# Sparse attention beside a short convolution: attention's products moved into the array's halves and spread over all dense products

## The chip, the core and the metric

One Trainium2 chip, of which the kernel uses one core. The metric is the device time of one execution in microseconds; lower is better. The figure given for a kernel is the median of its runs.

## The reference, cut to what matters

One token sequence of 512 tokens with 1024 channels passes through one layer. An RMS norm feeds one input projection whose columns are split: queries (8 heads of 64), six key and value tensors (2 key groups of 64 each), 24 gates, and five stretches of 512 columns for the attention's gate path and the convolution.

```python
h = rms_norm(x, norm_w)
q, kv, gate_logits, z_attn, conv_h, conv_b, conv_c, z_conv = split(h @ w_in)
kc, vc = compress(k_cmp), compress(v_cmp)     # 31 overlapping blocks of 32 tokens, an MLP with SiLU
for branch in (compressed, selected, window): # each with its own keys and values
    p = masked_softmax(q @ k.T / 8 + t5_bias(distance))      # causal
    o += sigmoid(gate[branch]) * (p @ v)
conv = conv_b * causal_conv3(conv_c * conv_h)
mixed = concat([o * silu(z_attn), conv * silu(z_conv)])
out = rms_norm(x + mixed @ w_out, final_norm_w)
```

With 512 tokens there are 8 blocks of 64 to select from and 16 may be selected, so the selected branch is full causal attention, and so is the window of 512. Four heads share the keys of a group. All data are float32.

## The kernel before, in words

**Products.** Each float32 product is made of parts: a number is split into a rounded part (hi) and the rest (lo), and three passes are summed, hi by hi, hi by lo and lo by hi. A dense product takes 128 channels by 128 output columns by 512 tokens; a chunk of 128 output columns has 8 of those, 24 passes (`chunk_task`, lines 281 to 285). The weights come by a DMA of 512 KB that SP issues, ScalarE writes hi (L272) and GpSimd lo (L274), and an evacuation that differs by chunk empties the PSUM bank.

**The stream.** Dense work is a list of tasks (`Stream`). `st.fill(ns)` puts so many nanoseconds of dense passes into TensorE's order, `st.run(n)` finishes the n-th task; loads run two tasks ahead of splits, and splits some tasks ahead of the products. TensorE's order is the order in the program. At the start SP's order and those of ScalarE, VectorE and GpSimd are written out by hand as well; afterwards the framework orders these from its own estimate of when each instruction can run. The stream's order is: attention's gate chunks (za), the convolution's gate chunks (zc), two key chunks (selected and window), the values in three tasks of 32 products with 280 columns, four query chunks, twelve convolution chunks, the convolution's half of the output projection, and for each block of 128 tokens the attention's half and the final norm.

**The start.** Two chunks, the keys and values to be compressed, follow the channel blocks of the tokens as they land; squares of the tokens give the norm (R). After them come the compression's first layer (`hid`, L731), its sum, and its second layer. The compression's weights are split into two tensors, tagged `mixc` and `T`.

**The bias table.** `T` holds for each of 128 queries the bias of 8 heads at 512 distances. VectorE writes a row for each head (`vr`), a DMA writes 32 copies of it to DRAM (`vrd`), and four loads of 512 KB read these back skewed (L719). The table has the tag `T`, and so it can be loaded only when the hidden layer has read the weights of that tag.

**Attention.** Query blocks of 128 tokens run in the order 3, 2, 1, 0, each with two key groups, each group with two units (selected and window; block 0 has both in one): 14 units. A unit does four heads of one key group. For each head the two score passes (L825) have 128 rows, which are hi and lo of the query one below the other, against a hi and a lo stack of keys that is stored twice. VectorE adds the bias to the scores in PSUM and finds the largest (L764) and leaves the result in memory; ScalarE takes the exponential there (L830) and `weigh` multiplies by the inverse sum and the gate and writes two float16 parts (L851, L852). A DMA transposes these for each head (L854, 56 in all), and the values' products (L892) have 512 columns (4 heads by 128 tokens) and 128 output rows (hi and lo of the values one below the other). The compressed probabilities are turned on VectorE in 32 by 32 blocks (L871) and enter by one product with 64 rows (`pch`, `vcs`). `merge` adds the two halves and applies the gate path. Scores of unit n + 2 are laid between the values of unit n, a step at a time, with dense passes between the steps (`FILL`, `FILL_S`, `FILL_END`).

PSUM has eight banks: 2 for dense products, 4 for scores, 2 for the attention's output.

Of the kernel before, what the change touches and what calls it, by code (L numbers as in the profile page):

```python
# [30 lines left out]
C_KC, C_VC, C_KS, C_KW = 512, 640, 768, 1024  # L31
C_VS, C_VW = 896, 1152
C_ZA, C_H, C_B, C_C, C_ZC = 1304, 1816, 2328, 2840, 3352
CHUNKS = ([C_KC, C_VC] + [C_ZA + 128 * j for j in range(4)] + [C_ZC + 128 * j for j in range(4)]
          + [C_KS, C_KW] + [128 * j for j in range(4)] + [C_B + 128 * j for j in range(4)]
          + [c + 128 * j for j in range(4) for c in (C_H, C_C)])
CH = {c: i for i, c in enumerate(CHUNKS)}
OUT_ORDER = (6, 7, 0, 1, 2, 4, 5, 3)
FILL_LEAD = 3600
ON_POOL = (1, 1, 0, 0)  # L40
BANKS = {'proj': 2, 'S': 4, 'o': 2}
NP = 4
LATER = (2400, 2400)
WOA_DVE = (2,)
WARM = 8
LAG = 1
# first loads: channels of the tokens and weights of the first two chunks; then the stream (z), small ones (c) and
# the first weights of the compression (w)
STARTS = (0, (C_VC, 0, 2), (C_KC, 0, 2), 1, 2, (C_KC, 2, 4), (C_VC, 2, 5), 3, 4, (C_KC, 4, 5), 5, (C_KC, 5, 8),
          (C_VC, 5, 8), 6, 7)  # L50
LOADS = 'zzcwwwwwwzww'
# the engine of each channel block's squares, and the additions that follow
SQ = 'VAVAVAAA'
ADDS = ((), ((0, 1, 'P'),), (), ((2, 3, 'V'), (0, 2, 'P')), (), ((4, 5, 'V'), (0, 4, 'V')), ((0, 6, 'P'),),
        ((0, 7, 'V'),))
LAST = 384
Z_POOL = 2
CLO_DVE = (2, 3)
HID_AT = 4
KV_AT = 1  # L60
AHEAD = 3
# how much of the dense products is laid between the steps of a unit, unit by unit
FILL = (5600, 4432, 1229, 59, 4584, 1731, 1954, 4314, 3026, 2165, 3883, 4401, 4462, 1860)
FILL_FIRST = 800
FILL_S = 500
FILL_END = 1300
NW = 8
NCST = 237       # packed small parameters
NCP = 32         # copies of the bias rows that the skewed read goes through
VG = 280         # v_slc | v_win | gates  # L70
# [20 lines left out]
TC = dict(schedule_with_timeline_sim=True)  # L91


@with_exitstack
def hybrid_kernel(ctx: ExitStack, tc: tile.TileContext, xt0, xt, x, wt, wv, w1k, w1v, cst, rbr, wo, fnw, out):
# [4 lines left out]
    raw = ctx.enter_context(tc.tile_pool(name="raw", bufs=3))  # L100
    whl = ctx.enter_context(tc.tile_pool(name="whl", bufs=3))
# [11 lines left out]
    wraws = {}  # L113

    def load_w(c, a, b):
        if not a:
            wraws[c] = raw.tile([128, 8, 128], F32, tag="wraw", name=f"wraw{c}")
        nc.sync.dma_start(out=wraws[c][:, a:b], in_=wt[CH[c]][:, a:b])
# [3 lines left out]
    nws = xts[0][:, 0:NW]  # L122

# [4 lines left out]
    def load_xt(k):  # L128
        if k == 0:
            nc.sync.dma_start(out=xts[0][:, 0:NW + S], in_=xt0)  # L130
        else:
            nc.sync.dma_start(out=xk(k), in_=xt[k - 1])

    for what in STARTS:
        if isinstance(what, int):
            load_xt(what)
        else:
            load_w(*what)
    rbt = one.tile([NH, NB], F32, tag="tmpa", name="rbt")
    csts = one.tile([128, NCST], F32, tag="pct", name="csts")  # L140
# [4 lines left out]
    rms, cws = kept[:, 0:1], kept[:, 1:13].rearrange("p (j i) -> p j i", i=3)  # L145

    # two unit matrices, one below the other
# [9 lines left out]
    # has the table loaded that the squares and the inverse root share  # L157
    nc.scalar.activation(sm.tile([128, 1], F32, tag="ss", name="first"), epsb, AF.Abs_reciprocal_sqrt)
    ones = one.tile([128, 128], F32R, tag="pch", name="ones")
    nc.vector.memset(f32(ones), 1.0)  # L160
    vr = one.tile([NH, S], F32, tag="convu", name="vr")
    vneg = one.tile([NH, 128], F32, tag="pc", name="vneg")
    nc.vector.memset(vneg, NEG)

# [17 lines left out]
    def part_w(c, a, b, w):  # L182
        t, ks = wraws[c], slice(a, b)
        if not a:
            w.extend(whl.tile([128, 8, 128], F32R, tag=n, name=f"{n}{c}") for n in ("whi", "wlo"))
# [379 lines left out]
    for j in range(4):  # L565
        chunk_task(128 * j, queries_to(j))
# [428 lines left out]
```

## Time and profile before

| what | us |
|---|---|
| median of 3 runs | 322.18 |
| lowest and highest run | 321.29, 322.49 |
| span of the profiled execution, first to last instruction | 319.6 |
| TensorE busy | 276.4 |
| VectorE busy | 225.9 |
| ScalarE busy | 169.6 |
| GpSimd busy | 171.3 |

The profile is of one execution, 319.6 us from its first to its last instruction; the runs are timed from outside and have a median of 322.18 us. The ends of matmuls are modelled: the record of a dense product lasts about 0.4 us although the next one starts 0.23 us after it, so the distance of starts is the pace. Times of one line of the program can be those of several shapes; the number behind x counts instructions. Idle time is put down to what ended it.

### The profile page before, as it was taken

To read this page: it belongs to the slowest core of one execution; us is meant where nothing else is said; L and a number is where in the kernel's file an instruction comes from. 1 tells how busy PE (TensorE), PEld (TensorE's weight loads), DVE (VectorE), ACT (ScalarE), POOL (GpSimd) and SP (SyncE) were. 2 spreads that over 40 slices of the span, in tenths; PEclk is the share of its full clock that TensorE was granted. 3 is DMA by queue.
4 is the path that set the end of the run, shared out by engine and by line. 5 is a ranking of instruction groups with operands and counts; after the bars stand their busy time and mean duration, and the time that the engine had idled before them with its cause. 6 is when DMAs were issued, how large, how long until landed. Compare 5 with 4: busy or idle time off the path is not lost. (4 is left out here: it accounts for less than half of the span.)

```text
span 319.6 us, 4299 instructions
## 1 busy us (share of the span) xinstructions
PE 276.4 (86%) x1248; PEld 212.4 (66%) x1248; DVE 225.9 (71%) x582; ACT 169.6 (53%) x357; POOL 171.3 (54%) x160
## 2 busy tenths in 40 slices
PE   6979998990699999999998998798959895999792
PEld 5647877870588977888776756575737563677482
DVE  3998968010115358368978988699699999899773
ACT  5915455200325437358485485854745756576562
POOL 3894744540664354436746455575765785234710
PEclk9889999997699999999999999999979999999999
DMA  6767421469532242242866895597566652343413
GB/s 197 280 192 284 132 66 66 53 119 218 181 97 72 82 170 79 66 132 44 194 131 144 149 196 167 133 162 162 160 141 98 195 186 49 49 71 99 115 68 131
DMA packets 55400, 42.59 MB, mean 133 GB/s; under 512 B 43984, under 2 KB 46416, under 8 KB 55376
## 3 DMA queue, kind: packets, MB, share of 16 engines
q1 hardware_dynamic: 55376, 42.31, 52.1%
q8 instruction: 10, 0.16, 0.2%
q14 instruction: 14, 0.11, 0.1%
HBM read 29.06 MB, written 2.75 MB: 100 GB/s over the span
## 5 line engine op out<-in xcount | busy, mean ns | idle before, releaser
L274 POOL TENSOR_TENSOR wlo<-wraw,whi 128x512 fp32r<-128x512 f32 x52 | 69.7, 1362 | 58.6 <-ACT whi L272 47.1
L281 PE MATMUL ps<-hhi,whi 128*128 128x512 f32 x208 | 84.4, 406 | 12.1 <-ACT zc L299 11.2
L283 PE MATMUL ps<-hlo,whi 128*128 128x512 f32 x208 | 83.3, 401 | 0.0
L285 PE MATMUL ps<-hhi,wlo 128*128 128x512 f32 x208 | 82.8, 398 | 0.4 <-POOL wlo L274 0.4
L281 PEld LDWEIGHTS ps<-hhi,whi 128*128 128x128 f32 x208 | 39.8, 191 | 21.9 <-ACT zc L299 11.6
L852 DVE SCALAR_TENSOR_TENSOR p<-P,den,p 128x512 f16<-128x512 f32 (+3 forms) x64 | 46.3, 763 | 4.8 <-ACT p L851 4.7
L830 ACT ACTIVATE P<-P,mx 128x512 f32<-128x512 f32 (+3 forms) x64 | 35.5, 556 | 24.7 <-DVE mx L764 21.4
L272 ACT CAST whi<-wraw 128x1024 fp32r<-128x1024 f32 x26 | 27.0, 1043 | 38.9 <-DMA wraw<-in_wt 20.3
L285 PEld LDWEIGHTS ps<-hhi,wlo 128*128 128x128 f32 x208 | 39.6, 190 | 9.0 <-POOL wlo L274 0.8
L283 PEld LDWEIGHTS ps<-hlo,whi 128*128 128x128 f32 x208 | 39.8, 191 | 8.0
L851 ACT ACTIVATE p<-P,den 128x512 f16<-128x512 f32 (+3 forms) x56 | 27.9, 566 | 16.8 <-issue 10.2
L825 PE MATMUL s<-K,Q 128*128 128x512 f32 (+5 forms) x112 | 33.4, 380 | 0.0
L892 PE MATMUL o<-pt,V 128*128 128x512 f16 x80 | 24.6, 390 | 7.2 <-DMA pt<-p 5.1
L764 DVE CUSTOM_DVE_ANT_0 P<-s,T 128x512 f32<-128x512 f32 (+3 forms) x64 | 29.6, 483 | 0.2
L825 PEld LDWEIGHTS s<-K,Q 128*128 128x128 f32 x112 | 21.1, 194 | 6.8 <-issue 1.5
L294 DVE TENSOR_TENSOR ps<-ps,R 128x512 f32<-128x512 f32 x10 | 7.0, 696 | 20.4 <-PE ps L285 20.3
L471 PE MATMUL pc<-wochi,mc 128*128 128x512 f32 x32 | 13.3, 415 | 5.9 <-DVE y L478 3.3
L892 PEld LDWEIGHTS <-V 128*128 128x128 f16 x80 | 4.6, 98 | 18.2 <-issue 13.8
L533 PE MATMUL po<-woa,mahi 128*128 128x512 f32 (+1 forms) x36 | 13.4, 372 | 1.0 <-DVE y L540 1.0
L535 PE MATMUL po<-woa,mahi 128*128 128x512 f32 (+1 forms) x36 | 13.9, 386 | 0.0
L537 PE MATMUL po<-woa,malo 128*128 128x512 f32 (+1 forms) x36 | 13.4, 372 | 0.0
L475 PE MATMUL pc<-wochi,mc 128*128 128x512 f32 x32 | 12.9, 403 | 0.0
(190 smaller groups left out, 526.2 us busy)
## 6 DMA issues: line engine op xcount, KB each, us to landing
wraw<-in_wt SPq DMA_DIRECT2D x26, 512.0 KB, 3.5
wo<-in_wo SPq DMA_DIRECT2D x8, 512.0 KB, 3.8
T<-vrd SPq DMA_DIRECT2D x4, 512.0 KB, 9.5
xt<-in_xt SPq DMA_DIRECT2D x7, 256.0 KB, 4.8
out<-z SPq DMA_DIRECT2D x3, 512.0 KB, 2.7
w1r<-in_w1k SPq DMA_DIRECT2D x4, 256.0 KB, 5.2
w1r<-in_w1v SPq DMA_DIRECT2D x4, 256.0 KB, 7.1
y<-in_x SPq DMA_DIRECT2D x2, 512.0 KB, 3.5
```

Source lines behind the costliest of these rows:

```text
L272: nc.scalar.copy(hi, t)
L274: nc.gpsimd.tensor_sub(lo[:, ks], t[:, ks], f32(hi[:, ks]))
L281: nc.tensor.matmul(ps, hi[:, k, :], hhi[:, k, :], start=(k == 0), stop=False)
L283: nc.tensor.matmul(ps, hi[:, k, :], hlo[:, k, :], start=False, stop=False)
L285: nc.tensor.matmul(ps, lo[:, k, :], hhi[:, k, :], start=False, stop=(k == 7))
L535: nc.tensor.matmul(ps, mh[:, k, :], woa[1][:, k, ns], start=False, stop=False)
L764: nc.vector.tensor_tensor_reduce(out=dst, in0=src, in1=bias, scale=-1.0, scalar=3e38, op0=ALU.add, op1=ALU.min, accum_out=mx)
L825: nc.tensor.matmul(o, Q[h][:, gr.qs], k, start=(p == 0), stop=(p == 1))
L830: nc.scalar.activation(P, P, AF.Exp, bias=ngm, scale=-1.0, accum_out=self.su[:, 4 * i + hh:4 * i + hh + 1])
L851: nc.scalar.mul(p16[:, i, 0], P, c)
L852: nc.vector.scalar_tensor_tensor(out=p16[:, i, 1], in0=P, scalar=c, in1=p16[:, i, 0], op0=ALU.mult, op1=ALU.subtract)
L892: nc.tensor.matmul(gr.ob, v, p, start=(gr.n_pv == 1), stop=(gr.n_pv == 4 * gr.qb + 5))
```

## The change

The rows and columns of the tensor engine's array are used in halves by attention. Keys and queries are stored once, with the channels of the two key groups on partitions 0 to 63 and 64 to 127; the columns of the query and attention gate chunks are put together accordingly (heads j and j + 4). A unit now does two heads of each group. A score takes three passes with 64 rows, and the two groups' passes alternate, into two banks. The scores stay in PSUM: bias, exponential and weighting read and write there, two heads at a time. Values are three passes with 64 output rows and 256 columns, the two groups in the two halves of the rows of one bank; the split of the values lies beside, not below. Compressed probabilities of all 8 heads of a query block are weighted together, written in float16 parts and turned by a DMA.

The order: four chunks (compressed values, compressed keys, selected keys, window keys) follow the tokens at the start. Then come values, queries, and from there attention's units, one whole unit of values and one of scores at a time, with 7.5 to 12 us of dense passes between units, over gate chunks, convolution, and output projection. Query blocks run in the order 3, 2, 0, 1. The bias table has its own space and eight loads, among the first weights in SP's order; 16 copies of the rows instead of 32. The hidden layers' weights use one tensor in turn, values first. SiLU is computed as x (1 + tanh(x/2)) with the half put into later factors. The output projection of the convolution does one block of tokens after the other with all four channel blocks rather than two blocks half and half; the last two channel blocks of the convolution's result stay in PSUM for their split. Four raw and four split weight buffers replace three.

```diff
-OUT_ORDER = (6, 7, 0, 1, 2, 4, 5, 3)
-FILL = (5600, 4432, 1229, 59, 4584, 1731, 1954, 4314, 3026, 2165, 3883, 4401, 4462, 1860)
+START = (VC, KC, KS, KW)
+OUT_ORDER = (0, 1, 2, 3, 6, 7, 4, 5)
+BLOCKS = (3, 2, 0, 1)
+NW_RING = 4
+FILL = {3: 12000, 2: 10000, 0: 7500, 1: 7800}
+BEHIND = {10: 27}
...
     def silu_to(dst, conv=False):
         def evac(ps):
-            nc.scalar.activation(dst(), normed(ps), AF.Silu)
+            nc.vector.tensor_mul(dst(), ps, R)
+            th = one.tile([128, S], F32, tag="tanh", name="th")
+            nc.scalar.activation(th, dst(), AF.Tanh, scale=0.5)
+            nc.vector.scalar_tensor_tensor(out=dst(), in0=th, scalar=1.0, in1=dst(), op0=ALU.add, op1=ALU.mult)
...
+    def keys_to(br, ps):
+        normed(ps)
+        nc.scalar.copy(K[:, 0, br, 32:], ps)
+        nc.vector.tensor_sub(K[:, 1, br, 32:], ps, f32(K[:, 0, br, 32:]))
...
+            nc.scalar.copy(q2[:, 0], ps)
+            nc.vector.tensor_sub(q2[:, 1], ps, f32(q2[:, 0]))
...
-            y = hy[j][:, 1, :]
-            nc.vector.tensor_mul(y, ps, y)
+            y = ps if j in CLO_DVE else hy[j][:, 1, :]
+            nc.vector.tensor_mul(y, ps, hy[j][:, 1, :])
...
         def mms(w):
             wcs[kp] = w
-            for tb in range(2):
-                yield from block(tb, (kp,))
-            if kp:
-                for tb in range(2, 4):
-                    yield from block(tb, (0, 1))
+            for tb in range(4) if kp else ():
+                yield from block(tb)
...
+    with tc.manual_schedule(engines={mybir.EngineType.SP}):
+        st.fetch(1)
+        nc.sync.dma_start(out=vrd.rearrange("b h i -> h b i"), in_=vr.unsqueeze(1).to_broadcast([NH, NCP, 640]))
+        st.fetch(2)
+        load_w1(1)
+        st.fetch(4)
+        load_bias(range(0, 4))
+        st.fetch(5)
+        load_bias(range(4, 8))
+        st.fetch(6)
+        load_w1(0)
...
+        def start_mm(k, part):
+            for i, c in enumerate(START):
+                wh, wl = (t[:, k % 2, i * 128:(i + 1) * 128] for t in whs[k // 2])
...
+    ROWS = [slice(0, 64), slice(64, 128)]
+    PARTS = ((0, 0), (1, 0), (0, 1))
...
+        def product(self, v, p):
...
+            for g in range(2):
+                nc.tensor.matmul(self.ob[ROWS[g], 0:256], v(g), p(g), start=(self.n_pv == 1),
+                                 stop=(self.n_pv == 6 * (self.qb + 1) + 1))
+        def merge(self):
+            h0 = 2 * self.jj
+            self.product(lambda g: vcs[:, g], lambda g: self.cmp.pt[:, 4 * g + h0:4 * g + h0 + 2])
+            zs = za[:, h0:h0 + 2, self.qs]
+            nc.vector.scalar_tensor_tensor(out=zs, in0=self.ob[:, 0:256].rearrange("p (j t) -> p j t", j=2), scalar=vdn,
+                                           in1=zs, op0=ALU.mult, op1=ALU.mult)
...
+            for j2 in range(2):
+                q = Q[2 * gr.jj + j2]
+                s = [bank("S", f"s{nm}{j2}{g}")[:, 0:nb * W].rearrange("p (b c) -> p b c", b=nb) for g in range(2)]
+                for n, (a, b) in enumerate(PARTS):
+                    for g in range(2):
+                        nc.tensor.matmul(s[g], q[ROWS[g], a, gr.qs], K[ROWS[g], b, brs[0]:brs[0] + nb, k0:k0 + W],
+                                         start=(n == 0), stop=(n == 2))
+                for g in range(2):
+                    P = s[g][:, :, c0:]
+                    self.P.append(P)
+                    for i in range(nb):
+                        ngm = self.ngm[:, i, j2, g:g + 1]
+                        neg_bias_max(P[:, i], P[:, i], T[:, 4 * g + 2 * gr.jj + j2, gr.off:512], ngm)
+                        nc.scalar.activation(P[:, i], P[:, i], AF.Exp, bias=ngm, scale=-1.0,
+                                             accum_out=self.su[:, i, j2, g:g + 1])
...
+                self.weigh(j2)
...
+            p16 = two.tile([128, 2, nb, 2, gr.L], F16, tag="P16", name=f"p16{nm}{j2}", bufs=3)
+            for g in range(2):
+                for i in range(nb):
+                    P, c = self.P[2 * j2 + g][:, i], d[:, i, g:g + 1]
+                    nc.scalar.mul(p16[:, g, i, 0], P, c)
+                    nc.vector.scalar_tensor_tensor(out=p16[:, g, i, 1], in0=P, scalar=c, in1=p16[:, g, i, 0],
+                                                   op0=ALU.mult, op1=ALU.subtract)
+            nc.sync.dma_start_transpose(out=self.pt[:, j2].rearrange("p g n t -> p (g n) t"),
+                                        in_=p16.rearrange("p g b a l -> p (g b a l)"))
+        def values(self):
+            gr = self.gr
+            n = gr.qb + 1
+            for i, br in enumerate(self.brs):
+                for kb in range(n):
+                    for a, b in PARTS:
+                        gr.product(lambda g: V[:, kb, 2 * br + g, a * DH:(a + 1) * DH],
+                                   lambda g: self.pt[:, :, g, (2 * i + b) * n + kb])
...
+    st.fill(4000)
+    units[0].scores()
+    st.run(6)
+    compressed_values()
+    st.fill(2000)
+    hidden(0)
...
+    units[1].scores()
+    st.fill(FILL[3])
+    for n in range(2, len(units) + 2):
...
+        u = units[n - 2]
+        u.values()
+        if u.brs[0] == 1:
+            u.gr.merge()
...
+        if n < len(units):
+            units[n].scores()
+            st.fill(FILL[units[n].gr.qb])
```

## Rows read from the trace of the kernel before

**Rows 1.** The page's part 1, whole span: engine, busy us (share of span), instructions.

```profile
PE 276.4 (86%) x1248; PEld 212.4 (66%) x1248; DVE 225.9 (71%) x582; ACT 169.6 (53%) x357; POOL 171.3 (54%) x160
```

**Rows 2.** Timeline of TensorE: start, duration, engine, line, operation, tiles, rows*columns, shape, count.

```profile
6.36 0.50 PE L604 MATMUL pkv<-hhi,whi 128*128 128x512 f32 x1 [1.74 <-ACT whi L186]
...
60.60 0.40 PE L281 MATMUL ps<-hhi,whi 128*128 128x512 f32 x1
...
65.40 0.39 PE L281 MATMUL ps<-hhi,whi 128*128 128x512 f32 x1
...
65.88 0.41 PE L757 MATMUL vcp<-csts,hs 128*31 128x64 f32 x4
66.22 0.50 PE L283 MATMUL ps<-hlo,whi 128*128 128x512 f32 x1
...
83.51 0.63 PE L283 MATMUL ps<-hlo,whi 128*128 128x512 f32 x1
83.94 0.63 PE L285 MATMUL ps<-hhi,wlo 128*128 128x512 f32 x1
...
181.42 0.39 PE L283 MATMUL ps<-hlo,whi 128*128 128x512 f32 x1
181.74 0.49 PE L892 MATMUL o<-pch,vcs 64*128 64x512 f32 x1
182.16 0.65 PE L825 MATMUL s<-K,Q 128*128 128x416 f32 x2
...
261.31 0.40 PE L825 MATMUL s<-K,Q 128*128 128x256 f32 x2
261.54 0.40 PE L475 MATMUL pc<-wochi,mc 128*128 128x512 f32 x1
```

**Rows 3.** Windows by stage: stretch, length, busy us (instructions) by engine, clock, DMA share, GB/s.

```profile
0.00:25.30 25.30, 19.80 (x66) 14.41 (x67) 18.47 (x19) 13.21 (x24) 17.25 (x24) 0.87 0.70 227
25.30:71.40 46.10, 44.59 (x215) 36.61 (x214) 26.56 (x62) 18.69 (x29) 24.90 (x25) 1.00 0.43 114
71.40:82.90 11.50, 0.34 (x2) 0.00 (x0) 0.19 (x1) 1.66 (x5) 0.54 (x1) 0.70 1.01 249
82.90:138.50 55.60, 55.01 (x277) 46.68 (x278) 24.17 (x47) 24.12 (x37) 29.06 (x23) 0.97 0.31 99
138.50:313.40 174.90, 156.60 (x693) 114.68 (x692) 155.02 (x449) 110.61 (x262) 99.06 (x88) 0.99 0.57 129
313.40:319.60 6.20, 0.05 (x1) 0.00 (x0) 1.49 (x4) 1.34 (x3) 0.55 (x1) 0.89 0.27 101
```

**Rows 4.** Waits of SP's DMA queue: who waited for whom, total us, times, longest.

```profile
SPq L719 <- DMA vrd<-vr: 11.3, 1, 11.3
```

**Rows 5.** DMA issues, whole span: tile, queue, kind, count, KB each, median us to landing.

```profile
T<-vrd SPq DMA_DIRECT2D x4, 512.0 KB, 9.5
...
pt<-p SPq DMA_TRANSPOSE x56, 3.1
```

**Rows 6.** Waits of TensorE, whole span: who waited for whom, total us, times, longest.

```profile
PE o L892 <- DMA pt<-p: 5.1, 2, 4.0
PE o L892 <- POOL pch L874: 4.2, 3, 2.0
PE pc L471 <- DVE y L478: 3.3, 3, 2.2
```

**Rows 7.** The page's part 5, costliest groups: busy us, mean ns, idle before them.

```profile
L852 DVE SCALAR_TENSOR_TENSOR p<-P,den,p 128x512 f16<-128x512 f32 (+3 forms) x64 | 46.3, 763 | 4.8 <-ACT p L851 4.7
...
L764 DVE CUSTOM_DVE_ANT_0 P<-s,T 128x512 f32<-128x512 f32 (+3 forms) x64 | 29.6, 483 | 0.2
...
L892 PEld LDWEIGHTS <-V 128*128 128x128 f16 x80 | 4.6, 98 | 18.2 <-issue 13.8
```

**Rows 8.** VectorE's groups by shape, whole span: busy us, mean ns, idle before.

```profile
L871 DVE STREAM_TRANSPOSE pct<-pc 32x128 f32<-32x128 f32 x32 | 9.6, 299 | 0.9 <-POOL pc L864 0.6
...
L904 DVE SCALAR_TENSOR_TENSOR mf<-o,small,ot 64x256 f32<-64x256 f32 x16 | 7.6, 476 | 3.2 <-ACT ot L899 2.8
```

More of the change, by code (lines that the diff above doesn't have):

```diff
@@ L367, in mms @@
             if k0 == 0:
-                pv.extend(bank("o" if t < 2 else "S", f"pv{t}") for t in range(4))
+                pv.extend(bank("proj" if t < 2 else "o", f"pv{t}") for t in range(4))
+                vf.append(two.tile([128, 4, 256], F32, tag="cvh", name="vf"))
             for tb in range(4):
@@ L676, in hybrid_kernel, with cast_w1, subtract_w1, by_tokens @@
+    w1s = {}
+    def cast_w1(kv):
+        w1s[kv] = one.tile([128, 2, 16, 128], F32R, tag="mixc", name=f"w1_{kv}")
+        for i in range(4):
+            nc.scalar.copy(w1s[kv][:, 0, 4 * i:4 * i + 4], w1p[kv][:, 4 * i:4 * i + 4])
+    def subtract_w1(kv, engine):
+        for i in range(4):
+            hi, lo = (w1s[kv][:, p, 4 * i:4 * i + 4] for p in range(2))
+            engine.tensor_sub(lo, w1p[kv][:, 4 * i:4 * i + 4], f32(hi))
+    def by_tokens():
         rsx = two.tile([128, 4, 32], F32, tag="mixf", name="rsx")
@@ L716, in load_bias, with hidden @@
-    def load_bias():
-        t = one.tile([128, NH, 512], F32, tag="T", name="T")
-        for p0 in range(0, 128, NCP):
-            nc.sync.dma_start(out=t[p0:p0 + NCP], in_=bass.AP(tensor=vrd.tensor, offset=vrd.offset + 127 - p0,
-                                                             ap=[[NH * 640 - 1, NCP], [640, NH], [1, 512]]))
-        return t
-    st.run(HID_AT)
-    hds = []
-    for kv in range(2):
-        hp = bank("S", f"hid{kv}")
+    hds, hss = {}, {}
+    def hidden(kv):
+        hp = bank("o", f"hid{kv}")
@@ L738, in hybrid_kernel, with hidden_sum @@
-    hss = []
-    for kv in range(2):
-        hp = bank("S", f"hsum{kv}")
+        nc.scalar.copy(hd, hp[:, 0:256])
+        hds[kv] = hd
+    def hidden_sum(kv):
+        hp = bank("o", f"hsum{kv}")
         for i in range(2):
@@ L743, in hybrid_kernel @@
                              stop=(i == 1))
-        hs = two.tile([128, 2, NC], F32, tag="P", name=f"hs{kv}", bufs=NP)
-        nc.scalar.activation(hs, hp[:, 0:2 * NC].rearrange("p (g c) -> p g c", g=2), AF.Silu)
-        hss.append(hs)
-    st.run(HID_AT + 2)
-    kp = bank("S", "kcp")
-    nc.tensor.matmul(kp[:, 0:2 * NC], w2kk, hss[0].rearrange("p g c -> p (g c)"), start=True, stop=True)
-    kpv = kp[:, 0:2 * NC].rearrange("p (g c) -> p g c", g=2)
-    for g in range(2):
-        kh, kl = KS[g][:, 0, 0, 0:NC], KS[g][:, 1, 0, 0:NC]
-        nc.scalar.copy(kh, kpv[:, g])
-        nc.vector.tensor_sub(kl, kpv[:, g], f32(kh))
@@ L755, in hybrid_kernel @@
-    vp = bank("S", "vcp")
-    for g in range(2):
-        nc.tensor.matmul(vp[0:NC, g * 64:(g + 1) * 64], hss[1][:, g, :], w2vs, start=True, stop=True)
-    vcf = one.tile([32, 2, 64], F32, tag="pct", name="vcf")
-    nc.vector.tensor_copy(vcf[0:NC], vp[0:NC, 0:128].rearrange("p (g d) -> p g d", g=2))
-    st.run(n_before)
+        hs = one.tile([128, 2, NC], F32, name=f"hs{kv}")
+        hv = hp[:, 0:2 * NC].rearrange("p (g c) -> p g c", g=2)
+        nc.scalar.activation(hs, hv, AF.Tanh, scale=0.5)
@@ L880, in values @@
-        def values(self, step):
-            gr = self.gr
-            if gr.ob is None:
-                gr.ob = bank("o", f"o{self.nm}")
-            if step is None:
-                mms = [(vcs[:, gr.g, :], self.pch)]
-            else:
-                i, kb = step
-                mms = [(V[:, kb, 2 * self.brs[i] + gr.g, :], self.pt[:, :, (2 * i + p) * (gr.qb + 1) + kb])
-                       for p in range(2)]
-            for v, p in mms:
-                gr.n_pv += 1
-                nc.tensor.matmul(gr.ob, v, p, start=(gr.n_pv == 1), stop=(gr.n_pv == 4 * gr.qb + 5))
```

724 lines of the change are left out of this document (333 added, 391 removed).

## The prediction

> **What bounds the kernel now.** I read the totals first. TensorE is busy 276.4 us of the 319.6 us span, and VectorE 225.9 [rows 1]. A matmul record ends about 0.16 us after the next one may start, so busy time is not work, and I count products by their pace instead. Twenty-one dense products of 512 columns lie between 60.60 and 65.40 us, which is 0.2286 us each [rows 2]. There are 864 dense products of that size (28 chunks of 24, 96 of the convolution's output, 96 of the attention's output): 197.5 us. Two score products of 256 columns take 0.23 us together, so columns set their price too and a load of 128 weight columns is covered at 0.115 us a product [rows 2].
>
> Next come the stretches [rows 3]. The reader is to see four kinds of loss. The start: 25.3 us for 50 products of 512 columns, which are worth 11.4. A hole: from 71.4 to 82.9 us nothing but DMA works, and the granted clock falls to 0.70 there and is 0.97 over the next stretch: after 11 us of rest the first products stand 0.43 us apart, the lower of the two levels (1.2 and 2.4 GHz) [rows 2]. The attention stretch, 138.5 to 313.4 us: TensorE idle 174.9 - 156.6 = 18.3 us, with VectorE busy 155.0 of 174.9, or 89%. The tail after the last product, 6.2 us. Between them, from 25.3 to 71.4 and from 82.9 to 138.5 us, TensorE waits 1.5 and 0.6 us while VectorE is busy about half the time: the gate paths run there with no attention beside them.
>
> The queue says why the hole is there [rows 4, 5]. SP stood 11.3 us for the write of the bias rows, then issued the four loads of the bias table, 9.5 us each to landing, and the weights of the chunk after next stood behind them. The table shares its space with a weight tensor of the compression and so could not come earlier. In the attention stretch the waits are for the turned probabilities (5.1 us), the turned compressed ones (4.2) and the outputs' additions on VectorE (3.3 and smaller ones) [rows 6].
>
> So the kernel is bound by TensorE's stream, with VectorE second in the one stretch into which all attention is pressed.
>
> **The hole.** After the change the table has its own space, its rows are built first on VectorE, and its eight loads stand in SP's order among the first weights, behind 1 MB of the compression's weights. What must land before the first scores is 2.1 MB of tokens, 2.1 of start weights, 1.2 of values' weights, 0.3 written for the table, 1.05 of compression weights, 2.1 of table, 1.05 of two query chunks: 9.9 MB, at the start's 227 GB/s [rows 3] 44 us. The first scores stand about 60 us into TensorE's order (31 start, 12.5 value products at their 280 columns, two query chunks of 5.5, hidden layer 1.9, then 4 more of dense fill). So I take the 11.2 us of idle as gone, with the 1.7 us that the clock costs afterwards (0.03 of 55.6): -12.9. Late next would be the last 1 MB of compression weights, wanted at about 66 us. Bounds: -12.9, and 0 if the wait only moves.
>
> **The start.** Now four chunks follow the tokens rather than two. The first product stood at 6.36 us [rows 2], behind a copy and a load that stay; 96 products at 0.2286 are 21.9, and the clock costs 3.3 (0.13 of 25.3), so the start ends near 31 us. Its 4.2 MB need 18.5 us at 227 GB/s, so TensorE is the limit. Before, the same work took 25.3 + 11.0 for the two key chunks later = 36.3: -5. Bounds -8 (no slow products) and +3 (the waits of before come for each of eight channel blocks as well).
>
> **The products of attention.** Scores: three passes with 64 rows each, the two key groups in the upper and lower half, instead of two passes of 128. Before: 32 x 0.2286 + 32 x 0.18 + 32 x 0.12 + 16 x 0.143 + 8 x 0.1 = 20.0 us (columns at the pace above). After: 168 products of 256 to 512 columns and 24 of 32. If the two of a pair run at once, a pair takes a column time, but its two loads of 128 columns may bind it: between 0.115 and 0.23 a pair by the 256-column rows; I take 0.2286 for the 24 pairs of 512 columns and 0.2 for the other 72, being nearest to two loads: 19.9. If they run one after the other: 48 x 0.2286 + 48 x 0.18 + 48 x 0.12 + 24 x 0.143 + 24 x 0.11 = 31.4.
>
> Values: 128 pairs of 256 columns and 64 output rows each, against 80 of 512 (18.3) and 8 with 64 rows at 0.51 (4.1), 22.4 in all. A pair costs 0.114 at the least, and at most 0.17, by four products of 31 weight columns that took 0.34 together [rows 2]; I take 0.14, the middle, as no row is nearer to either: 17.9. One after the other they are 29.3.
>
> Changing between shapes costs. The one product with 64 rows starts 0.32 us after its forerunner rather than 0.23, and the next starts 0.42 after it [rows 2]: 0.28 over two changes. The new order has three changes a unit in 14 units and two more, 44 x 0.14 = 6.2. Together: 19.9 + 17.9 + 6.2 - 20.0 - 22.4 = +1.6. Bounds: -11 (pairs at 0.115, half the changes' price), and +24.5 one after the other.
>
> That a pair runs at once no row of before can show, since it has no two neighbouring products in different halves; I take it because the two share neither rows (scores) nor output rows (values), nor a bank in the scores, and nothing in the order makes one wait. The Trainium skill (TensorEngine Tiling (Array Packing), "Key Properties") states that tiles work independently and load weights in parallel; by it the scores would be some 15 us, 5 below my sum; no run so far shows it.
>
> **The waits in the middle.** Idle in the three stretches is 20.4 us, and each of some 20 waits hides another 0.16 behind the late record end: 23.6. After the change units are spaced by 7.5 to 12 us of dense products and values lie two units behind their scores. VectorE loses much: the split of the probabilities reads PSUM instead of memory shared with GpSimd; as the other operation that reads PSUM at the same widths takes 483 ns against 763 [rows 7], 64 of them save 18. Turning the compressed blocks (9.6 us) goes to a DMA, and 16 merges (7.6) become 8 [rows 8]. The extra operation of each gate path (8 x 0.7) takes some back. That is about 30 less, and attention's work is laid over some 220 us instead of 175: 65 to 70% busy. So the additions and splits are no longer late; the transposes, 28 double ones and four small ones instead of 56, landed in 3.1 us before [rows 5] and get a slot of 10 or more. I leave 5 us of waits, about ten of the half-microsecond kind: -18.6. Bounds: 0 left, or all 23.6.
>
> The Trainium skill (TensorE: Matmul & The Clock Gate, Part 3, "The mechanism") says that a weight load overlaps a running product only when their row groups differ, and the halves of a value pair use all rows. Here the dense stream has the same rows in every product, each with its own load of 128 columns, and still goes at 0.2286 [rows 2], so the trace speaks against it. As a mechanism of this kernel it would add two loads to each value pair; see the third rival.
>
> **Costed at nothing.** Gate by tanh rather than SiLU, keys and queries in one copy, compression weights moved, output by whole token blocks, residual and output norm: on engines with room. The tail stays 6.2.
>
> **Sum.** 319.6 - 12.9 - 5 + 1.6 - 18.6 = 284.7 us of span. The median of the runs, 322.18, is 2.6 above the span, taken as what lies around it: 287.
>
> **Rivals.** (1) The halves run one after the other. For: no row shows a pair at once. Against: as above. +22.8: 310. (2) The hole stays as a wait at the first scores or the hidden layer: SP waits for the bias write and for raw buffers in order, as it did for 11.3 us [rows 4]; against, 16 us of slack. +11.2: 298. (3) Loads in value pairs uncovered: 2 x 0.058 (the values' 80 loads took 4.6 us [rows 7]) on 0.114 makes 0.23 a pair: +11.5, so 298. (4) Slower: a unit's four PSUM banks are now held from its scores until its probabilities are split, and the split needs one of three buffers that a transpose must have emptied. If split and transpose outlast a slot, TensorE, which works in order, waits at every unit. It decides once VectorE, ScalarE and the transpose need more than some 10.4 us a unit in the last blocks (7.8 fill at 1.06, plus 2.2). VectorE needs 4 x 0.97 = 3.9, with ScalarE about as much between, and the transpose 3.1 to 6.2, part of it in the next slot. Twelve units at the worst wait for a transpose of before, 4.0 [rows 6], are 48: 335.
>
> **Chances.** Forecast 0.60 (own range 275 to 298), rivals 0.13, 0.12, 0.05 and 0.10. About 0.5% is what a measurement can tell from no change. Faster holds for all but the fourth and some mixtures: 0.86; same 0.04; slower 0.10. The range for 8 in 10 runs from 268 (pairs cheaper, no waits) to 310.
>
> **What would show it.** No hole before the first scores; products of a pair starting nearly together, pairs at 0.2 us or less; the start's last product near 31 us; VectorE's total under 200 us; TensorE waits of 5 us in the middle. Wrong if pairs stand 0.23 apart at 512 columns, or scores wait for a bank.

## The result, and the profile after

The changed kernel takes 272.41 us (median of 4 runs, 271.73 to 272.81) against 322.32 us for the kernel before: a ratio of 0.846, with a 95% interval of 0.844 to 0.849. It is faster by 50 us, where 35 were forecast; the time lies in the range of 268 to 310 and just below the forecast's own range of 275 to 298.

The page of the changed kernel, part 1 (engine, busy us, share of the span, instructions), answers to [rows 1]:

```profile
span 269.6 us, 4430 instructions
...
PE 260.4 (97%) x1488; PEld 211.4 (78%) x1488; DVE 181.2 (67%) x481; ACT 152.4 (57%) x346; POOL 146.6 (54%) x143
```

TensorE goes from 86% of the span to 97%, VectorE loses 44.7 us of work. The windows by stage of the changed kernel (stretch, length, then busy us of PE, PEld, DVE, ACT, POOL, granted clock, DMA share, GB/s) stand against [rows 3]; the stages are the start, values and queries up to the first scores, to the end of the query chunks, the rest of the stream with attention laid through it, and the tail:

```profile
0.00:28.20 28.20, 26.90 (x114) 22.62 (x115) 15.20 (x39) 18.33 (x30) 18.69 (x27) 1.00 0.90 286
28.20:58.30 30.10, 30.10 (x184) 27.39 (x183) 22.57 (x47) 15.08 (x28) 20.75 (x23) 1.00 0.66 188
58.30:81.20 22.90, 22.90 (x135) 17.70 (x133) 17.46 (x41) 15.60 (x31) 15.52 (x12) 1.00 0.63 161
81.20:263.00 181.80, 180.28 (x1060) 143.68 (x1059) 124.38 (x351) 102.17 (x257) 91.10 (x80) 1.00 0.59 139
263.00:269.60 6.60, 0.22 (x2) 0.02 (x1) 1.62 (x5) 1.18 (x3) 0.55 (x1) 0.74 0.28 106
```

There is no stretch without products any more, the clock stays at its upper level until the tail, and VectorE is busy 68% of the long stretch (124.38 of 181.80) where it was 89%. The waits of TensorE over the whole span are these (who waited for whom, total us, times, longest):

```profile
PE warm L661 <- DVE ones L148: 1.1, 1, 1.1
PE pc L443 <- POOL woclo L430: 1.0, 2, 0.7
PE psza L261 <- DVE za L280: 0.5, 1, 0.5
PE pk_vc L681 <- DVE whis L667: 0.2, 1, 0.2
```

None is for attention; the 12.6 us of [rows 6] are gone. TensorE's timeline (start, duration, line, tiles, rows*columns, shape, count) shows the end of the start and one unit:

```profile
5.09 0.77 PE L681 MATMUL pk_vc<-hhi,whis 128*128 128x512 f32 x1 [0.23 <-DVE whis L667]
...
27.99 0.39 PE L685 MATMUL pk_kw<-hlo,whis 128*128 128x512 f32 x1
28.22 0.29 PE L346 MATMUL pv<-wvhi,hhi 128*128 128x280 f32 x1
...
96.15 0.39 PE L265 MATMUL psza<-hhi,wloza 128*128 128x512 f32 x1
96.47 1.50 PE L835 MATMUL o<-pt,V 128*64 128x256 f16 x24
97.90 1.67 PE L869 MATMUL s<-K,Q 64*128 64x512 f32 x12
99.50 0.50 PE L261 MATMUL psza<-hhi,whiza 128*128 128x512 f32 x1
```

The reader is to see that 24 value products take 1.43 us from their first start to the first score, and 12 score products 1.60 us to the next dense product. Twelve products of 512 columns one after the other would be 2.74 us at the dense pace. The single starts in the trace of this unit, in us, are:

```
values  96.470 96.474   96.603 96.606   96.713 96.716   96.821 96.825   96.931 96.934 ...
scores  97.901 97.904   98.239 98.243   98.475 98.478   98.706 98.710   98.941 98.944   99.172 99.176
```

A pair starts within 4 ns here. On average over the trace pairs follow each other at 0.109 us (values, 256 columns) and 0.233 us (scores, 512 columns); scores of 384 columns go at 0.176, of 256 at 0.120, and the compressed scores of 32 columns at 0.112.

### The profile page after: what moved, and what is told of

Read it like the earlier page. It is cut to its first block, busy times and chain, and to the rows that moved or that the text cites. A ratio compares the mean times of both kernels' runs of the same rounds, so it can differ in the third digit from the quotient of the medians.

```text
span 269.6 us, 4430 instructions
## 1 busy us (share of the span) xinstructions
PE 260.4 (97%) x1488; PEld 211.4 (78%) x1488; DVE 181.2 (67%) x481; ACT 152.4 (57%) x346; POOL 146.6 (54%) x143
## 4 chain that ended last, share of the span: by engine, by line
PE 59%; issue 3%; POOL 1%; ACT 1%; DVE 1%; POOLq 0%; DVEq 0%; ACTq 0%
PE o L835 6%; PE s L869 5%; PE psh L261 3%; PE psh L263 3%; PE psc L265 3%; PE pszc L265 3%; PE psb L263 3%; PE psh L265 3%; PE psb L261 3%; PE pszc L261 3%; PE psc L261 3%; PE psc L263 3%; PE pszc L263 3%; PE psb L265 3%; PE pc L443 3%
## 5 line engine op out<-in xcount | busy, mean ns | idle before, releaser
L878 ACT ACTIVATE s<-s,mx 128x512 f32<-128x512 f32 (+3 forms) x64 | 32.0, 501 | 37.3 <-DVE mx L760 37.0
L760 DVE CUSTOM_DVE_ANT_0 s<-s,T 128x512 f32<-128x512 f32 (+3 forms) x64 | 29.6, 520 | 12.4 <-PE s L869 11.6
L897 DVE SCALAR_TENSOR_TENSOR p<-s,den,p 128x512 f16<-128x512 f32 (+3 forms) x64 | 32.0, 545 | 6.0 <-ACT p L896 5.6
L896 ACT ACTIVATE p<-s,den 128x512 f16<-128x512 f32 (+3 forms) x64 | 29.8, 540 | 6.8 <-DVE den L767 3.8
L869 PE MATMUL s<-K,Q 64*128 64x512 f32 (+5 forms) x168 | 18.5, 352 | 0.0
L254 POOL TENSOR_TENSOR wlob<-wrawb,whib 128x512 fp32r<-128x512 f32 x8 | 10.9, 1386 | 11.8 <-ACT whib L252 11.8
L869 PEld LDWEIGHTS s<-K,Q 64*128 64x128 f32 x168 | 13.3, 185 | 3.8 <-issue 2.3
L835 PE MATMUL o<-pt,V 128*64 128x256 f16 x240 | 15.8, 276 | 0.0
L443 PE MATMUL pc<-woclo,mc 128*128 128x512 f32 x32 | 13.0, 405 | 1.0 <-POOL woclo L430 1.0
L261 PE MATMUL psza<-hhi,whiza 128*128 128x512 f32 x32 | 12.8, 401 | 0.5 <-DVE za L280 0.5
L878 ACT ACTIVATION_READ_ACCUMULATOR s<-s,mx 128x1 f32 x64 | 13.1, 204 | 0.0
L445 PE MATMUL pc<-wochi,mc 128*128 128x512 f32 x32 | 12.8, 399 | 0.0
L441 PE MATMUL pc<-wochi,mc 128*128 128x512 f32 x32 | 12.8, 399 | 0.0
```

The costliest lines, as they stand in the source:

```text
L254: nc.gpsimd.tensor_sub(lo[:, ks], t[:, ks], f32(hi[:, ks]))
L261: nc.tensor.matmul(ps, hi[:, k, :], hhi[:, k, :], start=(k == 0), stop=False)
L443: nc.tensor.matmul(ps, mc[0][:, 2 * kq + k, tsl], lo[:, k, :], start=False, stop=False)
L760: nc.vector.tensor_tensor_reduce(out=dst, in0=src, in1=bias, scale=-1.0, scalar=3e38, op0=ALU.add, op1=ALU.min, accum_out=mx)
L835: nc.tensor.matmul(self.ob[ROWS[g], 0:256], v(g), p(g), start=(self.n_pv == 1), stop=(self.n_pv == 6 * (self.qb + 1) + 1))
L869: nc.tensor.matmul(s[g], q[ROWS[g], a, gr.qs], K[ROWS[g], b, brs[0]:brs[0] + nb, k0:k0 + W], start=(n == 0), stop=(n == 2))
```

## Are the halves streams of their own?

Two accounts of the pairs are to be told apart. In the one, TensorE starts products in the order of issue, and a pair overlaps because its two are neighbours. In the other, the halves are two streams, and a product waits for its own half only. Three runs change the order of issue alone. The trace does not name the half of a product; below, the products are sorted into halves by the distance of their starts, which is one column time (the time in which the columns of one product stream, the paces above) within a half.

**Scores, three and three.** For each pair of banks, all three passes of one half before the three of the other.

```diff
-                for n, (a, b) in enumerate(PARTS):
-                    for g in range(2):
+                for g in range(2):
+                    for n, (a, b) in enumerate(PARTS):
                         nc.tensor.matmul(s[g], q[ROWS[g], a, gr.qs], ...
```

> The changed kernel, with the three passes of one key group's scores laid before the three of the other, so that neighbours lie mostly in the same half of the array; nothing else is changed. The scores' column time in pairs is 14.4 us (24 pairs at 0.2286, 24 at 0.179, 24 at 0.121, 12 at 0.143). Theory: products of different halves run at once and each waits only for its own half, in order of issue. Then of 12 products in a unit only three neighbours overlap, 9 column times instead of 6: +7.2 us, 279.6. Rival 1: nothing overlaps unless the passes alternate strictly: +14.4, 286.8. Rival 2: the pairs were cheap for another reason than running at once: no change, 272.4.

Measured: 271.43 us, ratio 0.843 (0.841 to 0.846): no change from the new kernel's 0.846. Starts in the order of issue would have cost time here, and that theory falls as it was put. The time alone would also fit the second rival; the starts speak against it. Half of a unit's twelve products have no neighbour in the other half, and yet the two halves run side by side: the first products of the two start at 97.233 and 97.243, though two others of the first half lie between them in the program.

**Values apart.** In each unit and branch, all value products of one half, then all of the other (3 to 12 in a row).

```diff
+            for g in range(2):
+                for n, (v, p) in enumerate(vps):
+                    nc.tensor.matmul(self.ob[ROWS[g], 0:256], v(g), p(g), start=(self.n_pv + n == 0), stop=False)
```

> The changed kernel, with all value products of one key group in a unit laid before those of the other; nothing else is changed. 116 pairs of 256 columns at 0.114 us are 13.3 us. Theory: the halves run at once, and only the two neighbours at the border of the groups overlap, so nearly all of it is paid a second time: +11.5 to +13, 285. Rival: the pairs were cheap for another reason: no change, 272.4.

Measured: 279.0 us, ratio 0.867 (0.864 to 0.869): 6.6 us slower, between the theory's 285 and the rival's 272.4. Now they do come apart, so the pairs were cheap because they run at once. The unit that took 1.43 us takes 2.33 in this run's timeline:

```profile
96.72 2.40 PE L834 MATMUL o<-pt,V 128*64 128x256 f16 x24
99.05 1.67 PE L877 MATMUL s<-K,Q 64*128 64x512 f32 x12
```

Of the first half's twelve products the ninth starts at 97.615; the second half's first starts at 97.621. Blocks of 3 products a half lost nothing in this run, 6 lost 0.25 us, 9 lost 0.57, 12 lost 0.90. This fits neither account as it stood: it looks like two streams with a look-ahead of about four products, so that n products of one half in a row cost n − 4 column times. The bound was read off these four lengths; whether it counts products, their weight loads or something else was not tried.

**Scores, six and six.** The test of that rule on other products: in each unit all six scores of one half first.

```diff
-                for n, (a, b) in enumerate(PARTS):
-                    for g in range(2):
-                        nc.tensor.matmul(s[g], ...
+            for g in range(2):
+                for j2 in range(2):
+                    for n, (a, b) in enumerate(PARTS):
+                        nc.tensor.matmul(ss[j2][g], ...
```

> The new kernel with one thing changed: in each unit all six score products of the one half are issued before all six of the other (in the new kernel they alternate; three and three cost nothing). Theory (the halves are streams of their own, and the second starts when the first has about four products left, as the value products showed): at six in a row two of six find the other half idle at either end, so each unit of 512 columns loses two column times of 0.23 us, and the score products, 14.4 us in pairs over all units, cost a third more: 4.8 us, so about 277 us against 272.4. Rival A (the look-ahead of score products has no such bound): 272 to 273. Rival B (they go wholly one after the other): 14 us more, 286. In the trace of a unit the second half's first score should start with the third of the first half by the theory, within some 10 ns of the first by A.

Measured: 277.42 us, ratio 0.862 (0.859 to 0.864): 5.0 us against the rule's 4.8. The closeness is partly luck: summed over the trace, the scores of all units take 6.5 us longer, and some 0.9 comes back in waits that this run doesn't have. The unit in its timeline:

```profile
97.19 1.50 PE L835 MATMUL o<-pt,V 128*64 128x256 f16 x24
98.62 2.23 PE L869 MATMUL s<-K,Q 64*128 64x512 f32 x12
100.78 0.50 PE L261 MATMUL psza<-hhi,whiza 128*128 128x512 f32 x1
```

2.16 us instead of 1.60 is 0.56, or two column times of 0.233 and 0.1 more: the second half now takes its own longer first step (0.337 from 99.197 to its next start). The second half's first score starts at 99.197, just behind the first half's third (99.190); the first half's other three, which stand ahead of it in the program, start at 99.422, 99.657 and 99.888.

## Where the hole came from

The next four runs change the kernel before, and only the bias table's way. The forecast held that the table could not come earlier because it shares its space. VectorE's order stood beside that: it built the rows only at 53.7 us, when the hidden layer had just read the shared space to its end (53.7 us too), and the write of the rows took until 66.9. The kernel before, VectorE and then SP's queue:

```profile
53.66 1.43 DVE L708 COPY vr<-rbt 8x399 f32<-8x399 f32 x16
...
55.20 0.30 SPq L713 DMA_DIRECT2D vrd<-vr  x1
66.95 2.10 SPq L719 DMA_DIRECT2D T<-vrd  x4
```

**Rows early.** Rows and their write right after the norm, amid VectorE's work on the gates; and the same with the table in its own space.

```diff
+        for b, i0, i1 in RUNS:
+            nc.vector.tensor_copy(vr[:, i0:i1], rbt[:, b:b + 1].to_broadcast([NH, i1 - i0]))
+        nc.vector.tensor_copy(vr[:, 512 - NB // 2:512], rbt[:, NB // 2:NB])
+        for a, b, t in ((0, S, vr), (S, 640, vneg)):
+            nc.sync.dma_start(out=vrd[:, :, a:b].rearrange("b h i -> h b i"), ...
```

> The kernel before, with one part of the change alone: VectorE builds the rows of the bias table, and SP writes them, before the compressed blocks rather than after the compression's weights; the table still shares its space with a weight tensor. Theory: SP's 11.3 us for the write of the rows was what kept the weights away, as the space came free at about 54 us: the hole shrinks by 9 to 13 us, 309 to 313. Rival: the shared space keeps the table late and the hole stays: 319 to 322.

> The same as the run with early rows, and the table has its own space as well and is loaded before the hidden layer (one sixteenth of the weights in another tile makes room). Theory (rows' order): within 2 us of the run with the shared space, 308 to 312. Rival (space): that run gains little and this one all of it, 309.

Measured: 319.78 us (ratio 0.992, 0.989 to 0.994) and 319.01 us (0.990, 0.987 to 0.994). The hole is gone in both and the time hardly moves: the rival's number. TensorE's waits in the first of these runs, which end at 53.5 and 40.8 us, name what took its place:

```profile
PE ps L285 <- POOL wlo L274: 4.1, 1, 4.1
PE ps L281 <- ACT za L299: 4.0, 1, 4.0
```

The granted clock falls to 0.70 and 0.66 in the two stretches of 10 us from 40 to 60 (windows of the same run):

```profile
40.00:50.00 10.00, 8.57 (x26) 6.57 (x26) 7.70 (x14) 5.42 (x9) 3.05 (x4) 0.70 0.35 59
50.00:60.00 10.00, 6.49 (x16) 5.16 (x17) 7.25 (x7) 3.61 (x6) 7.62 (x7) 0.66 0.29 90
```

The table's own space makes no difference here.

**Rows first.** Built while VectorE waits for the tokens anyway; the write stands with the small first loads; the space is shared as before.

```diff
+    rbt = one.tile([NH, NB], F32, tag="tmpa", name="rbt")
+    nc.scalar.dma_start(out=rbt, in_=rbr)
...
-                nc.sync.dma_start(out=rbt, in_=rbr)
+                for a, b, t in ((0, S, vr), (S, 640, vneg)):
+                    nc.sync.dma_start(out=vrd[:, :, a:b].rearrange("b h i -> h b i"), ...
```

> The kernel before with one thing changed: the bias values are loaded first, on ScalarE's queue, VectorE builds the rows of the table first, while it waits for tokens anyway, and their write to memory stands in SP's order with the small first loads. The table still shares its space with the compression weights. Two earlier runs that moved the rows amid VectorE's gate work lost the hole of 11 us and found 4 to 5 us waits on the gate path and a lowered clock instead, at 319 to 320 us. Theory (the hole is the chain of rows, write and table loads; the loss came back only because the rows stood in the way of VectorE's gate work): the hole shrinks to the table's loads after its space is free, at most 3 us, no new waits, 309 to 313 us. Rival (what the hole held up, the transfers of weights, is short in this stretch either way): new waits again, 317 to 321 us.

Measured: 316.01 us, ratio 0.981 (0.977 to 0.984), between the two. The hole is gone, and there are new waits, which GpSimd's timeline explains:

```profile
30.51 0.10 POOL L419 MEMSET cu<- 128x2 f32 x1 [6.13 <-DMA vrd<-vr]
33.31 0.20 POOL L804 MEMSET pc<- 128x128 f32 x1 [2.69 <-DMA vrd<-vneg]
33.47 1.27 POOL L275 TENSOR_TENSOR wlo<-wraw,whi 128x512 fp32r<-128x512 f32 x1
```

Two trivial fills of buffers that take over the space of the rows and of their fill value stand 8.8 us for the write, and the next split of weights behind them is what TensorE then waits 3.4 us for.

**Rows first, in a space not needed soon, written 9 us earlier.**

```diff
-LOADS = 'zzcwwwwwwzww'
+LOADS = 'zvzcwwwwwwzww'
...
-    vr = one.tile([NH, S], F32, tag="convu", name="vr")
+    vr = one.tile([NH, S], F32, tag="tmpa", name="vr")
```

> The kernel before with the rows first, as in the run at 316.0 us, and the two causes of its new waits taken away: there GpSimd had to wait 6.1 and 2.7 us for the bias rows' write before it could fill buffers that share their space, SyncE stood 13.3 us at the loads behind that write, and TensorE waited 3.4 and 2.2 us for GpSimd's splits and 1.1 us for a gate while its clock fell. Now the rows stand in a space that nothing else needs so early, and the write goes out right behind the first chunk's weights, 9 us earlier. Theory (the hole was that chain and nothing else; what came back was the place of the write): the new waits of 6.7 us go too, and some 1 to 2 us of clock: 308 to 311 us, no wait over 2 us between 30 and 100 us. Rival (this stretch lacks weights whatever the order, so that TensorE must wait somewhere before 100 us): 314 to 318 us.

Measured: 310.61 us, ratio 0.964 (0.962 to 0.966), a gain of 11.9 us. The other space and the earlier write were changed together; what each does was not tried. Its SP queue and its windows:

```profile
9.55 0.34 SPq L636 DMA_DIRECT2D vrd<-vr  x1
...
55.38 2.30 SPq L721 DMA_DIRECT2D T<-vrd  x4
```

```profile
30.00:60.00 30.00, 28.90 (x141) 23.87 (x140) 21.18 (x36) 13.48 (x21) 19.09 (x20) 1.00 0.49 157
60.00:70.00 10.00, 10.00 (x52) 8.36 (x51) 1.68 (x3) 1.77 (x4) 5.59 (x5) 1.00 1.05 240
70.00:82.90 12.90, 12.90 (x58) 10.68 (x57) 1.78 (x4) 4.68 (x8) 10.76 (x8) 1.00 0.29 93
```

The loads of the table are still issued only when the shared space is free (55.4 us; in the kernel before 66.9, when the write had landed), and TensorE waits for none of them. So the hole was the chain of rows, write and loads, with the rows' place in VectorE's order at its head. The gain holds a loss at the start: TensorE is busy 22.0 of the first 30 us here and 24.5 before.

## What the spacing and the rest are worth

The new kernel, with one thing changed in each.

**Pressed.** All gate chunks are finished before the compressed scores, and the dense passes between units are cut by a third. The second unit's scores then start at 118.8 us rather than 81.2, the last values stand at 266 rather than 256, and attention is pressed into a shorter stretch.

```diff
-FILL = {3: 12000, 2: 10000, 0: 7500, 1: 7800}
+FILL = {3: 8200, 2: 6800, 0: 5100, 1: 5300}
...
-    st.fill(3300)
+    st.run(15)
```

> The changed kernel, with all eight gate chunks finished before the compressed scores of the first query block, and the dense passes between the units cut to 68% (8.2, 6.8, 5.1 and 5.3 us): attention after its first unit is pressed into a later stretch, as before the change. Theory A (the waits in the middle went because VectorE has less work): VectorE is some 75% busy in the stretch and TensorE's waits stay under 3 us: 272 to 275.5. Theory B (they went because attention is spread over more of the stream): waits of 10 to 20 us come back: 282 to 292.

Measured: 283.33 us, ratio 0.879 (0.876 to 0.882): 10.9 us slower, as theory B has it. TensorE's waits:

```profile
PE s L869 <- DVE p L897: 5.3, 4, 3.7
PE pc L441 <- ACT mc L405: 3.2, 1, 3.2
```

The first line is the fourth rival, in small: scores wait for banks that the split still reads.

**Scores back in memory.** The bias step writes its result to memory as before, and exponential and split read it there.

```diff
-                    P = s[g][:, :, c0:]
+                    P = two.tile([128, nb, L], F32, tag="P", ...)
```

> The changed kernel, with the scores after bias and largest value written to memory, as before the change, rather than back into PSUM; exponential and split read them there. VectorE's split goes back from 545 to about 763 ns, +14 us on VectorE in all. Theory: TensorE's order leaves room for it, 271.5 to 273.5, with VectorE near 195 us. Rival: late splits make TensorE wait at units, 275 or more. Second rival: the score banks come free earlier, which gains up to 1 us.

Measured: 275.56 us, ratio 0.857 (0.852 to 0.861): 3.1 us slower, the rival's side. VectorE's groups of this run and of the new kernel (busy us, mean ns):

```profile
L898 DVE SCALAR_TENSOR_TENSOR p<-P,den,p 128x512 f16<-128x512 f32 (+3 forms) x64 | 45.8, 762 | 6.6 <-ACT p L897 6.1
L760 DVE CUSTOM_DVE_ANT_0 P<-s,T 128x512 f32<-128x512 f32 (+3 forms) x64 | 28.7, 483 | 11.8 <-PE s L869 11.4 <-issue 0.4
```

```profile
L760 DVE CUSTOM_DVE_ANT_0 s<-s,T 128x512 f32<-128x512 f32 (+3 forms) x64 | 29.6, 520 | 12.4 <-PE s L869 11.6
L897 DVE SCALAR_TENSOR_TENSOR p<-s,den,p 128x512 f16<-128x512 f32 (+3 forms) x64 | 32.0, 545 | 6.0 <-ACT p L896 5.6
```

The split is 762 ns from memory and 545 from PSUM; part of it comes back as waits of TensorE: 1.3 us for za (0.5 in the new kernel), and 1.1, 0.9 and 0.6 for T, K and vm, which the new kernel doesn't have.

**Two chunks at the start** rather than four; the two key chunks follow when all tokens are there.

```diff
+        for k in range(8):
+            for part in range(3):
+                start_mm(k, part, (2, 3))
```

> The changed kernel, with only two of the four start chunks (compressed values and keys) following the tokens; the two key chunks' 48 products come after the norm's product, from the same weights. Theory: with half the products in the tokens' phase TensorE waits for loads there, and the later 11.0 us are not hidden: the start's products end 3 to 7 us after 28.2 us, and the time is 275.4 to 279.4. Rival: the start was bound by something that both orders share: 272.4, or a lower clock in the pauses makes it worse than 7.

Measured: 275.66 us, ratio 0.856 (0.853 to 0.859): 3.3 us slower, at the low end of what was expected.

**SiLU on ScalarE again.**

```diff
-            nc.vector.tensor_mul(dst(), ps, R)
-            th = one.tile([128, S], F32, tag="tanh", name="th")
-            nc.scalar.activation(th, dst(), AF.Tanh, scale=0.5)
-            nc.vector.scalar_tensor_tensor(out=dst(), in0=th, ...)
+            nc.scalar.activation(dst(), normed(ps), AF.Silu)
```

> The changed kernel, with the gate paths by SiLU in one activation as before the change, instead of tanh and one more operation on VectorE; the factors of one half that go with tanh are taken out. ScalarE must now change its table between SiLU and the exponentials, which lie between the gate chunks: up to 16 loads of 1.28 us, +10 to +20 us on ScalarE, and VectorE loses 9. Theory: both have room, 272 to 274.5. Rival: late exponentials make TensorE wait, 276 to 285.

Measured: 272.71 us, ratio 0.847 (0.844 to 0.850): nothing, though ScalarE has 10 us more to do and VectorE 7 less.

**The convolution's output as before**, blocks half and half, and all channels' split from memory.

```diff
-            for tb in range(4) if kp else ():
-                yield from block(tb)
+            for tb in range(2):
+                yield from block(tb, (kp,))
+            if kp:
+                for tb in range(2, 4):
+                    yield from block(tb, (0, 1))
```

> The new kernel with the convolution's part undone: the output's token blocks in the order of before (two blocks opened with the first half of the channels, two whole ones after the second half) and the last channels' split from the copy in memory rather than from PSUM. Theory (engines have room there now, as the prediction costed this part at nothing): 271.5 to 273.5 us. Rival (the part keeps TensorE from waiting for the last channels of each chunk): 274 us or more, with waits for the split of the last channels.

Measured: 274.19 us, ratio 0.852 (0.849 to 0.855): 1.8 us more at the medians, and the intervals lie just apart (from 0.8494 here, up to 0.8485 there). Its waits have one of 2.6 us that the new kernel hasn't:

```profile
PE pc L443 <- DVE T L450: 2.6, 1, 2.6
```

That is the rival's side by the time, but not by its reason: the wait is for VectorE's addition that empties a bank of the output (L450), not for the split of the last channels. So the part costed at nothing is worth about 2 us; which of its two edits does it wasn't tried.

## Why the prediction was right, and where its sizes were off

The direction and the order of the terms held, and the main mechanism, halves that run at once, did too; what held the table and the bound by two loads were wrong. The forecast is 14.6 us too high, since the gains of the start, the products and the waits were all put too low. Counted from start to start of TensorE's products in both traces (a dense product at 0.227 us, what lies above it put down to the wait or change that stands there), the span loses 12.8 us of the hole, 8.2 at the start, 6.9 in attention's products, 21.0 of later waits and 1.1 of the rest.

**The hole (−12.9).** Right: no hole before the first scores, which stand at 58.62 us (about 60 was forecast), and −11.9 when only the hole is taken away. The reason given for it was partly wrong: the shared space, read to its end by 53.7 us, did not hold the table until 66.9; VectorE's late rows and their write did. The estimate of 44 us for 9.9 MB at 227 GB/s was on the slow side; the start moves 286 GB/s.

**The start (−5).** Its last product stands at 27.99 us, 31 was forecast, and values begin at 28.22: −8.1 against 36.3. The 3.3 us set down for a slow clock were wrong: four products stand 0.36 to 0.56 us apart, then TensorE keeps its upper level and is busy 26.9 of the 28.2 us. Of the gain, 3.3 us are the four chunks side by side, as the run with two shows; no run takes the rest apart.

**The products of attention (+1.6).** The term that was mis-sized most: −6.9. Score and value products with all changes of shape, the longer steps of the dense products beside them included, take 38.2 us where 44.0 were forecast. The 42.4 set down for before left most of its changes out; the same count gives 45.1 there. The pairs by themselves take 30.1 us where 37.8 were forecast. From 256 columns up, columns alone set a pair's price, 0.120 for 256 columns of scores where 0.2 was taken and 0.109 for values where 0.14 was: a pair's two weight loads run side by side as well. The compressed scores show it best, 0.112 us a pair with 32 columns: in the trace of before a single product of 64 columns with one such load (L809) stands 0.112 us from the next too. The changes between shapes cost a little more than the 0.42 a unit that was taken: dense to values 0.09 us, values to scores 0.09, then 0.10 within the first scores, 0.09 to dense, and the first dense product behind, 0.34 instead of 0.23, another 0.11.

The bound by two loads was the step that failed. The Trainium skill (TensorEngine Tiling (Array Packing), "Key Properties") spoke for the better number: it has tiles load and multiply independently, by which the scores were put at some 15 us. By the paces measured their 84 pairs take 14.8 us and the 12 compressed ones 1.3 (19.1 in all with the changes of shape up to the next product): the trace agrees. Another page of the Trainium skill (TensorE: Matmul & The Clock Gate, Part 3, "The mechanism") says that products start and end strictly in the order of issue; the run with six and six disagrees, as a product starts at 99.197 us before three of the other half that were issued ahead of it.

**The waits in the middle (−18.6).** 5 us were left for them; the view of waits has 1.5 us after the start. Counted by starts, with what hides behind the late record ends, 2.0 of 23.0 us are left: −21.0. The pressed run ties about half of that to the spacing: closer units bring back 10.9 us, with the wait for banks. The run with the scores back in memory ties 3.1 us to VectorE's lighter split; the rest was not isolated. VectorE's total was to fall by about 30 to under 200, though the pieces named there add up to 26; it fell by 44.7. The split from PSUM saves 14.0 us (64 times 763 less 545 ns), 18 were taken. VectorE's groups in the two traces name more: 9.6 for the turned blocks, 6.9 for keys and queries in one copy, 5.1 for the merges with their gate, 4.2 for compression weights that are split elsewhere; the extra operation of the gate paths takes back 9.4 where 5.6 was set down.

**The rivals.** The halves one after the other (310): refuted, by pairs that start 4 ns apart. The hole as a wait (298): refuted. Uncovered loads in value pairs (298): refuted, 0.109 a pair. Held banks (335): not in this order; the pressed run shows that it begins as soon as the units stand a third closer. The tail was to stay at 6.2 and is 6.6.

## What to carry to other kernels

Two products that use different halves of the array, by rows or by output rows, cost one column time together, loads included, from 256 columns up here; lay them so that few products of one half stand in a row (three cost nothing here; four by the rule, which no run tried). Judge a queue's wait by all that stands in its chain: here the rows' place in VectorE's order was the cause, and a buffer's next user on another engine brought part of the loss back until the buffer was another and the write stood earlier. Latency-bound work spread evenly through a dense stream hides where the same work pressed together doesn't.

## What the runs showed of the hardware

The two halves behave as separate streams with a look-ahead of about four products across their border, in scores (64 rows) as in values (64 output rows): blocks of 3 cost nothing in either, 6, 9 and 12 values of 256 columns cost 0.25, 0.57 and 0.90 us, and 6 scores of 512 columns 0.56. That issue order is not start order between the halves had not been expected. Nor had it that VectorE's bias step, which reads PSUM either way, is slower when it also writes there (520 against 483 ns), which takes back 2.4 of the 14 us that the split gains.
